# A ring of half pieces, a fifth pair by seven products, and results added to the residual by transfers, in one encoder layer

## The chip, the cores and the metric

The kernel runs on one core of a Trainium2 chip. Its engines work side by side, each through its own list of instructions in order: TensorE (PE, with PEld for its weight loads), VectorE (DVE), ScalarE (ACT), GpSimd (POOL) and SyncE (SP), which here only issues DMA transfers. The metric is the device time of one execution in microseconds (us), as a median of several runs. The profile is one execution, recorded instruction by instruction.

## The reference, cut to what matters

One encoder layer for 256 tokens of width 2048, float32 throughout:

```
h = rms_norm(x);  proj = h @ w_in                  # queries, keys, values, two gates
merged = sigmoid(ga) * (ya @ w_branch_a) + sigmoid(gb) * (yb @ w_branch_b)   # ya, yb: two attentions
x = x + merged @ w_out
hf = rms_norm(x);  g = dwconv3(hf @ w_ffn_gate)
x = x + (gelu(g) * (hf @ w_ffn_up)) @ w_ffn_down   # inner width 5632
x = x + sigmoid(rms_norm(x) @ w_ple_gate) * (p @ w_ple_proj)
out = rms_norm(x)
```

The change bears mostly on the product with `w_ffn_down`, 5632 rows by 2048 columns.

## The kernel before, in words

**Weights.** All weights are cut into blocks of 128x128, put on the host into the order in which they are used (`_stream`), and packed 16 to a *piece* of 1 MB; 263 pieces stream in on SP's queue (`load`, L198) into a ring of three buffers named `raw` (24 KB of each partition). `split_to` (L205) turns eight blocks at a time into two tensors for the matmuls: ACT rounds them to `whi` (L217), and DVE subtracts to get the remainder `wlo` (L218). Each has four buffers, and `split_to` runs three or four groups ahead of PE. A product is then three matmuls, high by high, high by low and low by high (L267 to L269, L311 to L313), which keeps float32's accuracy; the narrower products use two (L244, L245).

**Order.** The layer is a list of *jobs* (`_plan`): projections, attention, the `o` job in four quarters, then twice (for each half of the inner width) 22 gate and 22 up jobs and two *down* jobs `d0` or `d1`, one for each half of the 2048 columns; then four small `pp` jobs and four `pg` jobs. `at(...)` hangs small work (transposes, normalisation) on a step of a job, and `run_due` issues it there. A scheduler at compile time then fixes each engine's order from its own estimates, so that instructions of an engine can be moved against each other; `keep` holds an instruction in the order of the program.

**Down jobs.** A down job (`seven_product`, L288) takes its 22 rows of blocks in 11 pairs; a pair is one piece of weights, 2 rows by 8 columns of blocks, and two token halves. A normal pair takes eight block products of 512 columns, 24 matmuls. A *saved* pair takes seven, in the way of Strassen and Winograd, 21 matmuls. For it `combine` (L222) makes four differences of weight blocks on DVE (L229, L233, L234; the tile `spare`), so that such a pair has 28 blocks to split instead of 16, in four groups; and `add_up` makes four sums of activations (tiles `a32`, `s32`, then `shl`) after the eighth up job, for all four pairs in one go. `ORDER` puts four saved pairs (0 to 3) between seven normal ones: 4, 0, 5, 1, 6, 2, 7, 3, 8, 9, 10. When the last saved pair is done, `spread_sums` (L721) takes four PSUM banks into the residual with one ACT copy and eight DVE additions (L728); at the job's end `joined` (L776) adds the other four banks to the residual, each by a DVE instruction, and in `d1` ACT squares each quarter (L781) for the next norm.

**After the down jobs.** `flip` transposes the residual on PE (L745) and scales it into two halves on ACT (L367) and DVE (L368). `pp` copies its results on ACT (L702). Before `pp` job 2 the last gain is loaded by ACT's queue (L876). `gate` (L787 to L792) closes each quarter; `finish` sums the squares (L798), scales the sum (L387), raises it to -0.5 on POOL (L389), multiplies and stores (L802 to L807).

Of the kernel before, what the change touches and what calls it, by code (L numbers as in the profile page):

```python
# [111 lines left out]
ORDER = [4, 0, 5, 1, 6, 2, 7, 3, 8, 9, 10]  # L112
SAVED = 4
# [8 lines left out]
def _stream():  # L122

    blocks = [(j[2], j[4] + k, j[3]) for k in range(KC) for j in _JOBS[:FIRST]]
    for _, _, name, n, k0, count in _JOBS[FIRST:]:
        if isinstance(n, tuple) and len(n) == 8:
            for m in ORDER:
                if m < SAVED:
                    _SEVEN.add(len(blocks))
                blocks += [(name, k0 + 2 * m + e, c) for e in range(2) for c in n]  # L130
# [11 lines left out]
def _splits():  # L142

    subs = [(int(a), n, None) for a, n in zip(np.cumsum([0, 1, 2, 4, 4]), (1, 2, 4, 4, 5))]
# [13 lines left out]
def _encoder(ctx: ExitStack, tc, xt, pt, cols, table, onehot, mask, ident_in, last_gain, wts, xrows, out):  # L158
# [36 lines left out]
    def load(r, a=0, b=PIECE):  # L195
        if a == 0:
            raws[r] = wpool.tile([P, PIECE, P], F32, name="raw", bufs=3)
        nc.sync.dma_start(raws[r][:, a:b, :], wts[r].rearrange("p (b n) -> p b n", n=P)[:, a:b, :])  # L198
        state["raw"] = r + 1

    def load_all(i):
        while state["raw"] < min(i, _NPIECES):
            load(state["raw"])

    def split_to(i):  # L205
        while state["sub"] < min(i, len(_SUBS)):
            s = state["sub"]
            a, n, part = _SUBS[s]
            r, o = divmod(a, PIECE)
            load_all(r + 3)  # L210
            src = raws[r][:, o:o + n, :]
            if part is not None:
                src = combine(src, part)
# [8 lines left out]
    def combine(b, part):  # L222

        if part == 0:
            state["turn"] = turn = 1 - state.get("turn", 1)
            state["t"] = held["spare"][:, turn * PIECE * P:(turn + 1) * PIECE * P].rearrange("p (b n) -> p b n", n=P)
            four = b.rearrange("p (q b) n -> p q (b n)", q=4)
            t13 = state["t"][:, :8, :].rearrange("p (q b) n -> p q (b n)", q=2)
            nc.vector.tensor_tensor(t13, four[:, 1::2], four[:, :2], op=ALU.subtract)  # L229
            return b[:, 8:, :]  # L230
        if part == 1:
            t1, t2, t4 = (state["t"][:, c:c + 4, :] for c in (0, 8, 12))
            nc.vector.tensor_tensor(t2, b[:, 12:, :], t1, op=ALU.subtract)  # L233
            nc.vector.tensor_tensor(t4, b[:, 8:12, :], t2, op=ALU.subtract)  # L234
            return state["t"][:, :8, :]
        return state["t"][:, 8:, :] if part == 2 else b[:, :4, :]
# [51 lines left out]
    def seven_product(i, still, sums, tags, done):  # L288
# [14 lines left out]
        for m in ORDER:  # L303
            for name in ("p2", "p3", "p4") + (("p1", "p5", "p6", "p7") if m < SAVED else ("p2", "p3", "p4", "c22", "c22")):
# [14 lines left out]
        for m in ORDER:  # L319
            b = state["at"]  # L320
            s, _ = _SUB_OF[b]
            if m < SAVED:
# [7 lines left out]
            for e, steps in enumerate(each):  # L330
                if m >= SAVED or e % 2 == 0:
# [8 lines left out]
            if m == SAVED - 1:  # L340
# [96 lines left out]
    hba = big.tile([P, QH, AW], F32, name="hba", tag="b0", bufs=1)  # L437
    hbb = big.tile([P, BH, BW], F32, name="hbb", tag="b1", bufs=1)
# [4 lines left out]
    order = [(0, 1), (0, 0, 1), (0, 1, 3), (0, 3, 7), (1, 2), (0, 7, 11), (0, 11, PIECE), (2, 3)]  # L443
# [57 lines left out]
    def bias(h0, n):  # L501

        if h0 < QH:
            dst, lines = hba[:, h0:h0 + n, :], [[1, P]]
# [25 lines left out]
    def scores(heads, y):  # L530
# [17 lines left out]
        a, step = (hba[:, h, :], P) if n == 1 else (hbb[:, h - QH, :], 1)  # L548
# [75 lines left out]
    def after(job, i, acc, u=None):  # L624
# [66 lines left out]
        elif kind == "u":  # L691
# [3 lines left out]
            v = held["a32"][:, f, :] if f < 2 * SAVED else u  # L695
            nc.vector.tensor_tensor(v, u, held.pop(("gelu", n)), op=ALU.mult)
            halves(held["act"][:, f, :], v)
            if f == 2 * SAVED - 1:
                add_up()
# [4 lines left out]
    def add_up():  # L704

        a = held["a32"].rearrange("p (m e) (t n) -> p m e t n", e=2, t=2)
        a11, a12, a21, a22 = a[:, :, 0, 0], a[:, :, 1, 0], a[:, :, 0, 1], a[:, :, 1, 1]
        s = held["s32"]
# [4 lines left out]
        hi, lo = held["shl"][:, 0], held["shl"][:, 1]  # L713
        for c in (slice(0, 2), slice(2, 4)):
            nc.scalar.activation(hi[:, c], s[:, c], AF.Copy)
            nc.vector.tensor_tensor(lo[:, c], s[:, c], hi[:, c].bitcast(F32), op=ALU.subtract)
# [4 lines left out]
    def spread_sums(n, bank):  # L721

        q = [[res[:, t, (2 * n + c) * W4:(2 * n + c + 1) * W4] for c in range(2)] for t in range(2)]
        u = held["ff"].tile([P, W4], F32, name="sq4")
        v = held["ff"].tile([P, W4], F32, name="gate", bufs=2)

        def add(dst, a, b):
            nc.vector.tensor_tensor(dst, a, b, op=ALU.add)  # L728

        nc.scalar.activation(u, bank["p1"], AF.Copy)  # L730
        add(q[0][0], u, q[0][0])
        add(u, bank["p6"], u)
        add(v, bank["p7"], u)
        add(u, bank["p5"], u)
        add(q[1][0], v, q[1][0])
        add(v, bank["p5"], v)
        add(q[0][1], u, q[0][1])
        add(q[1][1], v, q[1][1])
# [22 lines left out]
    def merge(n, e, m):  # L761
# [6 lines left out]
        hi, lo = (held["merged"][k // SUB][:, k % SUB:k % SUB + 2, c:c + T] for c in (0, T))  # L768
# [3 lines left out]
    def joined(n, t, acc, scale, parts):  # L772
# [6 lines left out]
        if parts is not None:  # L779
# [204 lines left out]
```

## Time and profile before

| | us |
|---|---|
| median of 3 runs (lowest to highest) | 1480.47 (1480.2 to 1480.53) |
| the profiled execution | 1477.88 |
| its span, from the first to the last instruction | 1476.1 |
| PE busy in it | 1462.2 |
| DVE, ACT, POOL busy | 1065.5, 760.5, 3.7 |
| down jobs of the first half, first to last matmul's start | 888.99 to 1004.46 |
| down jobs of the second half | 1249.22 to 1365.34 |

The profile names an engine, the line of the kernel, and output and inputs by tile. The granted TensorE clock is 0.997 of full speed. In the rows of the timeline the first number is the start in us from the span's start, the second the duration; the bracket at the end gives idle time of that engine just before and what ended it. A busy time of PE counts modelled ends, since matmuls overlap; the distance between the starts of two matmuls is their pace.

### The profile page before, as it was taken

What the parts mean: (1) busy time and instruction counts of PE and PEld (TensorE: products, weight loads), DVE (VectorE), ACT (ScalarE), POOL (GpSimd) and SP (SyncE); (2) the same over time, 40 slices, a digit from 0 to 9 for tenths busy, and PEclk for the clock granted to TensorE, in tenths of its full rate; (3) what the DMA queues carried; (4) which work ended last, traced back from release to release, by engine and by line L of the source; (5) the groups of instructions that cost most, each with busy time, mean ns of one, the idle gap of its engine ahead of it and who ended that gap; (6) DMA issues with size and microseconds to landing.
All of it is one profiled execution on the core that took longest, in us unless ns stands there. A gap on an engine that the chain in (4) does not pass through costs nothing. (4 is left out here: it accounts for less than half of the span.)

```text
span 1476.1 us, 19530 instructions
## 1 busy us (share of the span) xinstructions
PE 1462.2 (99%) x7570; PEld 1248.4 (85%) x7570; DVE 1065.5 (72%) x1530; ACT 760.5 (52%) x1072; POOL 3.7 (0%) x9
## 2 busy tenths in 40 slices
PE   9999999999999999999999999999999999999997
PEld 8888888888888888888888888888888888888886
DVE  7686664664554555568898888887889888898565
ACT  7465444444444444555555555554555555655643
POOL 0000000000000000000000000000000000000000
PEclk9999999999999999999999999999999999999998
DMA  9644444445555554545455454555455454555552
GB/s 321 245 156 171 169 171 171 171 177 194 204 197 192 202 207 180 198 171 197 178 196 196 180 196 171 205 223 192 183 196 189 184 198 172 201 200 216 211 188 97
DMA packets 46375, 282.88 MB, mean 192 GB/s; under 512 B 5124, under 2 KB 9988, under 8 KB 14028
## 3 DMA queue, kind: packets, MB, share of 16 engines
q1 hardware_dynamic: 44268, 277.31, 50.8%
q10 hardware_dynamic: 2016, 4.33, 1.1%
q8 instruction: 59, 0.97, 0.2%
q14 instruction: 32, 0.26, 0.0%
HBM read 279.49 MB, written 2.14 MB: 191 GB/s over the span
## 5 line engine op out<-in xcount | busy, mean ns | idle before, releaser
L218 DVE TENSOR_TENSOR wlo<-raw,whi 128x1024 fp32r<-128x1024 f32 (+2 forms) x519 | 622.1, 1201 | 355.6 <-ACT whi L217 352.4
L217 ACT ACTIVATE whi<-raw 128x1024 fp32r<-128x1024 f32 (+2 forms) x519 | 541.1, 1043 | 605.5 <-PE acc L269 224.9
L244 PE MATMUL acc<-mov,whi 128*128 128x512 f32 x1840 | 641.9, 393 | 0.3 <-DVE mov L368 0.3
L245 PE MATMUL acc<-mov,wlo 128*128 128x256 f32 x1840 | 512.8, 279 | 0.0
L244 PEld LDWEIGHTS acc<-mov,whi 128*128 128x128 f32 x1840 | 344.7, 187 | 77.6 <-DVE mov L368 0.6
L245 PEld LDWEIGHTS acc<-mov,wlo 128*128 128x128 f32 x1840 | 346.7, 188 | 0.4
L268 PE MATMUL acc<-wlo,mov 128*128 128x512 f32 (+1 forms) x512 | 196.5, 384 | 0.5 <-DVE wlo L218 0.5
L267 PE MATMUL acc<-whi,mov 128*128 128x512 f32 (+1 forms) x512 | 196.8, 385 | 0.0
L269 PE MATMUL acc<-whi,mov 128*128 128x512 f32 (+1 forms) x512 | 196.4, 384 | 0.0
L267 PEld LDWEIGHTS acc<-whi,mov 128*128 128x128 f32 x512 | 96.7, 189 | 19.3 <-DVE wlo L218 0.8
L268 PEld LDWEIGHTS acc<-wlo,mov 128*128 128x128 f32 x512 | 96.7, 189 | 19.0 <-DVE wlo L218 0.9
L269 PEld LDWEIGHTS acc<-whi,mov 128*128 128x128 f32 x512 | 96.7, 189 | 18.8
L312 PE MATMUL acc<-wlo,act 128*128 128x512 f32 x272 | 106.3, 391 | 0.8 <-DVE wlo L218 0.8
L311 PE MATMUL acc<-whi,act 128*128 128x512 f32 x272 | 106.1, 390 | 0.0
L313 PE MATMUL acc<-whi,act 128*128 128x512 f32 x272 | 105.9, 389 | 0.0
L312 PEld LDWEIGHTS acc<-wlo,act 128*128 128x128 f32 x272 | 51.1, 188 | 12.0 <-DVE wlo L218 1.7
L311 PEld LDWEIGHTS acc<-whi,act 128*128 128x128 f32 x272 | 51.1, 188 | 10.7
L313 PEld LDWEIGHTS acc<-whi,act 128*128 128x128 f32 x272 | 51.1, 188 | 10.5
L267 PE MATMUL acc<-whi,merged 128*128 128x512 f32 x128 | 50.6, 396 | 0.0
L269 PE MATMUL acc<-whi,merged 128*128 128x512 f32 x128 | 49.9, 390 | 0.0
L268 PE MATMUL acc<-wlo,merged 128*128 128x512 f32 x128 | 49.8, 389 | 0.0
L217 ACT ACTIVATE whi<-spare 128x1024 fp32r<-128x1024 f32 x32 | 33.7, 1054 | 27.0 <-PE acc L313 26.2
(177 smaller groups left out, 1373.0 us busy)
## 6 DMA issues: line engine op xcount, KB each, us to landing
raw<-in_wts SPq DMA_DIRECT2D x251, 1024.0 KB, 4.8
raw<-in_wts SPq DMA_DIRECT2D x12, 512.0 KB, 7.4
x<-in_xrows ACTq DMA_DIRECT2D x8, 256.0 KB, 5.3
x<-in_xt SPq DMA_DIRECT2D x13, 128.0 KB, 6.6
hbb<-hold SPq DMA_DIRECT2D x3, 514.0 KB, 6.3
hba<-hold SPq DMA_DIRECT2D x2, 768.0 KB, 7.1
end<-in_last_gain ACTq DMA_DIRECT2D x1, 1024.0 KB, 4.8
out<-x ACTq DMA_DIRECT2D x2, 384.0 KB
```

What stands on the lines that cost most here:

```text
L217: nc.scalar.activation(hi, src, AF.Copy)
L218: nc.vector.tensor_tensor(lo, src, hi.bitcast(F32), op=ALU.subtract)
L244: nc.tensor.matmul(acc, hi[:, o, :], m, start=first, stop=False, skip_group_check=True)
L245: nc.tensor.matmul(acc[:, T:], lo[:, o, :], m[:, :T], start=False, stop=last, skip_group_check=True)
L267: nc.tensor.matmul(acc, xh, hi, start=(k == 0), stop=False)
L268: nc.tensor.matmul(acc, xh, lo, start=False, stop=False)
L269: nc.tensor.matmul(acc, xl, hi, start=False, stop=(k == n - 1))
L311: nc.tensor.matmul(acc, xh, hi, start=(e == 1), stop=False)
L312: nc.tensor.matmul(acc, xh, lo, start=False, stop=False)
L313: nc.tensor.matmul(acc, xl, hi, start=False, stop=(e == uses[name]))
```

## The change

It has these parts:

1. **The ring.** `raw` becomes six buffers of half a piece (8 blocks, 512 KB). Every piece is loaded by two transfers, and a buffer is free when its own eight blocks are split. `split_to` asks for half pieces five ahead of the one that it splits, six in the later groups of a saved pair. In a saved pair the second row's blocks now come first in the stream, so that the first half piece (`b2`) is one whole group; `combine` makes all four differences at the first group, from both halves, as four DVE instructions of 512 columns. Its target `spare` becomes two tiles of one piece each. The first piece is split as 1, 2, 5, 4, 4 blocks instead of 1, 2, 4, 4, 5.
2. **A fifth saved pair** in both `d0` jobs and in the first `d1` job, in the order 5, 0, 6, 1, 7, 2, 8, 3, 4, 9, 10. The second `d1` job keeps four. `add_up` now runs pair by pair, on tiles of the new ring `row` (seven buffers of 128x512).
3. **Results by transfers.** `spread_sums` copies one bank on ACT, adds three others on DVE with four instructions, and gives its four results to `to_residual`: a DMA issued by POOL that adds a 128x512 tile to the residual in SBUF. In the three jobs with five saved pairs the four results at the job's end go the same way, after a copy by ACT. In the last job two of the first four results and all of the last four are still added by DVE. The squares of the first `d1` job move to step 10 of the second, and all squares are kept in program order on ACT.
4. **Room.** The bias tables and the tile `merged` are cut differently between two buffers (`b0` smaller, `b1` larger).
5. **Small work.** Transposes of `merge` and `flip` that came at two steps come at one (steps 3, or 17 and 19; after the last down job, step 0 of the second `pp` job and step 1 of the third). The last gain is multiplied by the root of 2048 on DVE before `pp` job 3; the sum of three quarters' squares is made early (`so_far`), and `finish` adds the fourth's with one instruction in place of the sum and the scaling.

The diff, cut to its core:

```diff
+SAVED = 5
+SPLIT = 4
+ROWS = 7
+def _pairs(kind, c):
+    if kind == "d1" and c == 1:
+        return [4, 0, 5, 1, 6, 2, 7, 3, 8, 9, 10], 4
+    return [5, 0, 6, 1, 7, 2, 8, 3, 4, 9, 10], 5
...
     def load(r, a=0, b=PIECE):
-        if a == 0:
-            raws[r] = wpool.tile([P, PIECE, P], F32, name="raw", bufs=3)
-        nc.sync.dma_start(raws[r][:, a:b, :], wts[r].rearrange("p (b n) -> p b n", n=P)[:, a:b, :])
-        state["raw"] = r + 1
+        src = wts[r].rearrange("p (b n) -> p b n", n=P)
+        for h in range(a // SUB, -(-b // SUB)):
+            c, d = max(a - h * SUB, 0), min(b - h * SUB, SUB)
+            if c == 0:
+                raws[2 * r + h] = wpool.tile([P, SUB, P], F32, name="raw", bufs=6)
+            nc.sync.dma_start(raws[2 * r + h][:, c:d, :], src[:, h * SUB + c:h * SUB + d, :])
+            state["raw"] = 2 * r + h + 1
...
-            load_all(r + 3)
+            load_all(h + 6 + bool(part))
...
-    def combine(b, part):
+    def combine(b2, b1, part):
         if part == 0:
+            t = state["t"] = held["spare"][turn]
+            (b21, b22), (b11, b12) = [[b[:, :4, :], b[:, 4:, :]] for b in (b2, b1)]
+            t1, t3, t2, t4 = (t[:, c:c + 4, :] for c in range(0, PIECE, 4))
+            for dst, p, q in ((t1, b12, b11), (t3, b22, b12), (t2, b22, t1), (t4, b21, t2)):
+                nc.vector.tensor_tensor(dst, p, q, op=ALU.subtract)
+        return (b2, state["t"][:, :8, :], state["t"][:, 8:, :], b1[:, :4, :])[part]
...
+    def to_residual(n, t, c, a):
+        keep(nc.gpsimd.dma_start(quarter(n, t, c), a, accum_op=ALU.add))
+    def spread_sums(n, bank, end):
+        u = row()
         nc.scalar.activation(u, bank["p1"], AF.Copy)
+        to_residual(n, 0, 0, u)
+        last = u
+        for name in ("p6", "p7"):
+            v = row()
+            nc.vector.tensor_tensor(v, bank[name], last, op=ALU.add)
+            last, u = v, last
+        u, v = u, last
+        to_residual(n, 1, 0, v)
+        w = row()
+        nc.vector.tensor_tensor(u, bank["p5"], u, op=ALU.add)
+        nc.vector.tensor_tensor(w, bank["p5"], v, op=ALU.add)
+        for t, a in enumerate((u, w)):
+            if end:
+                q = quarter(n, t, 1)
+                nc.vector.tensor_tensor(q, q, a, op=ALU.add)
+            else:
+                to_residual(n, t, 1, a)
...
-                joined(2 * n + c, t, acc[name], 1.0, held["ss2"] if kind == "d1" else None)
+                if kind == "d1" and n:
+                    joined(2 * n + c, t, acc[name], 1.0, held["ss2"])
+                else:
+                    a = row()
+                    nc.scalar.activation(a, acc[name], AF.Copy)
+                    to_residual(n, t, c, a)
+                    if kind == "d1":
+                        at((i + 1, 10), squares_of, c, t, held["ss2"])
```

More of the change, by code (lines that the diff above doesn't have):

```diff
@@ L718, in summed, with row @@
     def summed(m, e):
         return [held["shl"][:, c, e, m, :] for c in range(2)]
[L721 to L738, printed above, removed]
+    def row():
+        return held["ff"].tile([P, W4], F32, name="row", bufs=ROWS)
```

143 lines of the change are left out of this document (75 added, 68 removed).

## The prediction

> **What bounds the kernel now.** I read the page first, then the stretches of the down jobs, then the single waits. The page's first part:
>
> ```profile
> span 1476.1 us, 19530 instructions
> ...
> PE 1462.2 (99%) x7570; PEld 1248.4 (85%) x7570; DVE 1065.5 (72%) x1530; ACT 760.5 (52%) x1072; POOL 3.7 (0%) x9
> ```
>
> PE is the bound, but its busy time is modelled, so the pace is read from the starts. Inside a down job (a quarter of L311 to L313):
>
> ```profile
> 913.74 0.39 PE L312 MATMUL acc<-wlo,act 128*128 128x512 f32 x1
> ...
> 919.63 0.39 PE L311 MATMUL acc<-whi,act 128*128 128x512 f32 x1
> 920.45 0.50 PE L312 MATMUL acc<-wlo,act 128*128 128x512 f32 x1 [0.43 <-DVE wlo L218]
> 920.79 0.39 PE L313 MATMUL acc<-whi,act 128*128 128x512 f32 x1
> ```
>
> From 913.74 to 919.63 lie 26 steps: 0.2265 us a matmul of 512 columns, whatever its row says of its own length. The next two steps are 0.82 and 0.34: 0.71 lost to a wait for DVE. So time goes only in two ways: fewer matmuls, or fewer waits of PE. The waits list names the large waits in the down jobs and what is behind them:
>
> ```profile
> DVE spare L229 <- DMA raw<-in_wts: 3.9, 5, 1.4
> ...
> PEld acc L312 <- DVE wlo L218: 1.7, 2, 0.9
> ```
>
> There are two such stops of PE. What led to the first stands in DVE's timeline:
>
> ```profile
> 904.62 1.23 DVE L229 TENSOR_TENSOR spare<-raw 128x1024 f32<-128x1024 f32 x1
> 905.76 0.69 DVE L218 TENSOR_TENSOR wlo<-raw,whi 128x512 fp32r<-128x512 f32 x1
> 906.36 0.69 DVE L233 TENSOR_TENSOR spare<-raw,spare 128x512 f32<-128x512 f32 x1
> 907.08 0.69 DVE L234 TENSOR_TENSOR spare<-raw,spare 128x512 f32<-128x512 f32 x1
> 907.69 3.58 DVE L218 TENSOR_TENSOR wlo<-raw,whi 128x1024 fp32r<-128x1024 f32 x3
> 911.19 1.22 DVE L218 TENSOR_TENSOR wlo<-spare,whi 128x1024 fp32r<-128x1024 f32 x1
> 913.44 1.23 DVE L218 TENSOR_TENSOR wlo<-spare,whi 128x1024 fp32r<-128x1024 f32 x1 [1.03 <-ACT whi L217]
> 916.10 1.23 DVE L229 TENSOR_TENSOR spare<-raw 128x1024 f32<-128x1024 f32 x1 [1.44 <-DMA raw<-in_wts]
> ```
>
> DVE was free at 914.66, but the piece of the next saved pair had not landed until 916.10; everything behind it on DVE moved back, and PE stood at 920.45. The piece takes the buffer of the normal pair, whose two remainders are the first two of the three at 907.69. Overlapped, a 1024-wide DVE step costs 1.14 us (904.62 to 905.76), a 512-wide one 0.60, so that buffer was free at 907.69 + 2 x 1.14 = 909.97. The landing row of line 198 in this stage fits:
>
> ```profile
> DMA to landing us min/median/max: 4.7/4.8/6.1
> ```
>
> 909.97 + 6.1 is 916.1. A last large stop stands where the gate job starts:
>
> ```profile
> 1378.67 1.08 ACT L702 ACTIVATE end<-acc 128x512 f32<-128x512 f32 x2
> 1379.62 1.07 ACT L217 ACTIVATE whi<-raw 128x1024 fp32r<-128x1024 f32 x1
> ...
> 1380.72 1.23 DVE L218 TENSOR_TENSOR wlo<-raw,whi 128x1024 fp32r<-128x1024 f32 x1 [1.44 <-ACT whi L217]
> ```
>
> ```profile
> 1381.10 0.39 PE L267 MATMUL acc<-whi,mov 128*128 128x512 f32 x1
> 1382.00 0.50 PE L268 MATMUL acc<-wlo,mov 128*128 128x512 f32 x1 [0.52 <-DVE wlo L218]
> 1382.34 0.40 PE L269 MATMUL acc<-whi,mov 128*128 128x512 f32 x1
> ```
>
> Steps of 0.90 and 0.34 there: 0.79 lost, because ACT's rounding of those weights stood behind two copies of line 702.
>
> **Fewer matmuls.** A normal pair takes 8 x 3 = 24 matmuls, a saved one 7 x 3 = 21. Counts over the two jobs of the first half:
>
> ```profile
> L312 PE MATMUL acc<-wlo,act 128*128 128x512 f32 x136 | 53.2, 391 | 0.8 <-DVE wlo L218 0.8
> ...
> L312 PE MATMUL acc<-wlo,shl 128*128 128x512 f32 x32 | 12.4, 389 | 0.0
> ```
>
> 168 here, as many on L311 and L313: 504, or 4 x 21 + 7 x 24 = 252 a job. With five saved pairs it is 249. Three jobs: nine matmuls, 9 x 0.2265 = **2.04 us**, certain if PE stays fed.
>
> **Does DVE keep up?** Busy time of the two jobs, and of a stretch of the gate and up jobs (after the window: its length, PE, PEld, DVE, ACT, POOL, clock, DMA share, GB/s):
>
> ```profile
> 889.00:946.00 57.00, 56.57 (x251) 46.48 (x250) 49.63 (x57) 30.87 (x33) 0.00 (x0) 1.00 0.55 202
> 946.00:1004.00 58.00, 57.62 (x254) 47.39 (x253) 48.50 (x53) 30.19 (x31) 0.00 (x0) 1.00 0.54 203
> ```
>
> ```profile
> 660.00:880.00 220.00, 220.00 (x1272) 193.97 (x1271) 184.57 (x325) 115.36 (x182) 0.00 (x0) 1.00 0.52 191
> ```
>
> A new saved pair costs DVE four 512-wide steps, two of them dependent (0.72 as 906.36 to 907.08), so 2.6; then three remainders of 1.14 and one of 0.60: 6.6 in all, against 2.3 for the normal pair it replaces: +4.3. The sums after the last saved pair fall from nine to four (-3.0), and four additions into the residual leave DVE (-2.4). Sum -1.1: about 48.5 of 56.3 us. On ACT, 1.5 more roundings (1.6 us) and four copies that replace DVE's additions:
>
> ```profile
> L776 DVE TENSOR_TENSOR x<-acc,x 128x512 f32<-128x512 f32 x6 | 3.9, 684 | 1.1 <-PE acc L313 1.1
> ...
> L730 ACT ACTIVATE sq<-acc 128x512 f32<-128x512 f32 x2 | 1.2, 582 | 0.0
> ```
>
> 4 x 0.58 makes 34.8 of 56.3 for ACT. Both keep cover. In the gate and up jobs the sums of a pair come one pair at a time. Each of four 128x128 additions lies between 0.16 (the 128x1 rows of the tail below) and 0.68 (the 512-wide row); I take 0.25, which with a 512-wide remainder is 1.7 us a pair, 8.5 for five; the block it replaces was 4 x 0.68 + 2 x 1.2 = 5.1. DVE is idle for 35 of 220 us there, so I count nothing; at 0.68 it would be 17 in 250, still covered.
>
> **The ring.** The second half piece of a saved pair now waits only for its own 512 KB. Rows:
>
> ```profile
> raw<-in_wts SPq DMA_DIRECT2D x251, 1024.0 KB, 4.8
> raw<-in_wts SPq DMA_DIRECT2D x12, 512.0 KB, 7.4
> x<-in_xrows ACTq DMA_DIRECT2D x8, 256.0 KB, 5.3
> ...
> out<-gate SPq DMA_DIRECT2D x2, 256.0 KB, 2.5
> ```
>
> Between 2.5 for 256 KB and 4.8 for 1 MB, 512 KB is some 3.3 us, an estimate (7.4 was at the start, with many queued). The first half's buffer is free at 908.83, the second's at 909.97: landed by 913.3 (914.8 at 4.8). DVE reaches the combination at 914.66, so neither makes it wait. Both stops then go: 0.71 and, for the second, which has the same cause by the waits list, about 0.65: **-1.35**. What is late next is PE's own pace. SP issues twice as many transfers, 44 in 116 us at about 0.35 each: hidden.
>
> The Trainium skill ("DMA: Bandwidth & Descriptors", section "Rules for kernel authors") asks for 1 MiB or more in one DMA, which speaks against half pieces. Its fit, 2.0 us plus bytes at 436 GB/s, gives 3.2 for 512 KB, and the 4.8 row for 1 MB lies near its 4.4; by the rule alone the sum would be that of rival 4.
>
> **Two saved pairs in a row.** Pairs 3 and 4 are adjacent: DVE needs 6.6 us for pair 4 while PE spends 21 x 0.2265 = 4.76 on pair 3. That is 1.85 short, and DVE's lead covers it if the combination is issued early, as L229 is (ahead of the previous pair's last remainder at 905.76). Bounds 0 and 3 x 1.85 = 5.5; nearest to the timeline is little, **+0.3**.
>
> **Results by transfer.** 26 transfers of 256 KB, issued by POOL, which is otherwise idle; eight in each of three jobs, two in the last. Issue and landing aren't in this trace; by the 256 KB rows one takes 2.5 to 5.3 us. They add 2.1 MB to some 11.5 MB a job, a DMA share of 0.55 to perhaps 0.7. First to wait are ACT's four squares at step 10 of the last job: from the last saved pair until then PE has two normal pairs (10.9), then three normal and two saved ones (25.8): 36.7 us for eight transfers, 4.6 each if one after another. At 3.3 they are done: **0**. The ring of seven rows is reused a job later, and is covered likewise.
>
> **Start of the gate job.** Flips one and three move forward by up to one small job, so their transposes and ACT copies no longer stand before the rounding; against it DVE gains the multiplication of the last gain. 2048 wide, by
>
> ```profile
> L806 DVE TENSOR_SCALAR x<-x,rr 128x768 f32<-128x768 f32 x2 | 1.2, 612 | 0.0
> ...
> L802 DVE TENSOR_SCALAR gate<-gate,rr 128x512 f32<-128x512 f32 x2 | 1.0, 487 | 1.5 <-POOL rr L389 1.5
> ```
>
> 0.125 more for 256 columns gives 1.2 us (0.6 to 2.4). It also waits for its 1 MB transfer, and may hold up remainders behind it. Bounds -0.79 and +2; I take half the stop, **-0.40**. Elsewhere flips and merges are regrouped, with as many transposes: nothing.
>
> **Tail.**
>
> ```profile
> 1469.41 0.16 DVE L798 TENSOR_REDUCE sum<-marks 128x1 f32<-128x4 f32 x1
> 1469.60 0.16 DVE L387 TENSOR_SCALAR rv<-sum 128x1 f32<-128x1 f32 x1
> ```
>
> One small addition in place of both: **-0.19**, on the path. More queues to close at the end: 0 to 0.5, I take **+0.1**. Chunks at the start are cut otherwise, with the same bytes ahead of the same blocks: nothing.
>
> **Sum.** -2.04 - 1.35 + 0.30 - 0.40 - 0.19 + 0.10 = -3.58. The profiled execution took 1477.88, span 1476.06; it becomes 1474.3. The runs' median is 2.59 above the profiled time; keeping that, 1480.47 - 3.6 = **1476.9 us**.
>
> **Rivals.**
> 1. *The matmuls go, the waits stay* (half pieces land no earlier, or an equal stop comes elsewhere). For it: DVE is 86% busy in these jobs. Against: the 1.4 us between 914.66 and 916.10. -2.04 - 0.19 = 1478.2.
> 2. *Adjacent saved pairs starve PE*, up to +5.5: 1477 to 1482.4, most likely 1479.5. For it: 6.6 against 4.76. Against: the order seen at 904.62.
> 3. *Slow transfers make it slower.* Place: ACT's squares in the last job, behind which weight roundings queue; PE lives on four buffers of 6 to 12 matmuls, some 6 us. From about 5.3 us a transfer, one after another, this decides (8 x 5.3 = 42.4 against 36.7 + 6); at 7 us PE stands 13 us: 1490. For it: no row of such a transfer exists, and 5.3 is a measured row for this size. Against: that row's eight loads ran beside weights, and transfers to different quarters need not go one after another. The Trainium skill ("SBUF — State Buffer", "Who interferes with whom") says that descriptors for DMAs issued from GpSimd are held up while VectorE runs in a two-port mode, but not by tensor_tensor; by that rule the down jobs, whose DVE rows are all TENSOR_TENSOR, would escape, and no run here shows it yet.
> 4. *Half pieces move one after another*: 2 x 3.3 a piece against 5.2 us of matmuls, 1.4 late on each of 263 pieces: about 1840. Against it is a stretch near the start, in which the twelve transfers of 512 KB were the largest:
>
> ```profile
> 10.00:20.00 10.00, 9.18 (x52) 7.78 (x53) 8.00 (x12) 8.72 (x13) 0.00 (x0) 1.00 1.02 391
> ```
>
> 391 GB/s, more than twice what 512 KB in 3.3 us give (159): they run side by side.
>
> **How the numbers follow.** This kernel's measurement can tell about 0.2% from no change: below 1477.51 is faster, above 1483.43 slower. Forecast 0.53: with every gain and no loss the sum is -2.04 - 1.35 - 0.79 - 0.19 = -4.4, 1476.1, and 0.6 below that stands for terms taken as nothing: 1475.5; above, 1478.0 (mostly below the bound), rival 1 0.18, rival 2 0.14, rival 3 0.13, rival 4 0.02. Faster: 0.42 of the forecast, 0.03 of rivals 1 and 2: 0.45. Same: 0.11 + 0.16 + 0.13 = 0.40. Slower: 0.15. The range from 1475.5 to 1482.4 holds all but rivals 3 and 4.
>
> **What would show it.** 249 matmuls in three jobs; no wait of DVE for raw in them, and no PE step over 0.4 us; DVE about 48 us a job; the transfers' landing below 4.6 us; step sizes around the first remainder of pair 4; the start of the gate job. It is wrong if PE's waits grow past 2 us anywhere, most of all behind ACT's squares.

## The result and the profile after

| | us |
|---|---|
| before, median of 6 runs beside it (lowest to highest) | 1480.22 (1477.75 to 1480.53) |
| after, median of 6 runs (lowest to highest) | 1488.14 (1485.87 to 1490.53) |
| ratio after to before, 95% interval | 1.0058 [1.0045, 1.0071] |
| the profiled execution after, its span | 1489.59, 1487.7 |
| down jobs of the first half, before and after | 115.5 and 118.6 |
| down jobs of the second half, before and after | 116.1 and 125.0 |

The change makes the kernel slower by 0.58%, 8.6 us by the ratio. The forecast was 1476.9, the range ended at 1482.4. The profiled executions lie further apart (11.7 us) than the medians, since that of before was near its quickest run and that of after above its median; in what follows stops are counted in the profiled executions and sizes are taken from the ratios.

The page of after, its totals, queues and transfers:

```profile
span 1487.7 us, 20288 instructions
...
PE 1463.7 (98%) x7561; PEld 1246.8 (84%) x7561; DVE 1071.0 (72%) x1577; ACT 771.7 (52%) x1096; POOL 26.7 (2%) x35
...
q1 hardware_dynamic: 80412, 277.33, 56.9%
q0 software_dynamic: 3744, 6.82, 2.5%
...
raw<-in_wts SPq DMA_DIRECT2D x514, 512.0 KB, 4.7
x<-row POOLq DMA_DIRECT2D x26, 256.0 KB, 7.5
```

PE has 7561 matmuls where it had 7570: nine fewer, as intended, at the same pace of 0.227 us. DVE's total is 1071.0 after 1065.5. So no engine has much more to do, and the time is in waits. After's list of waits (engine and line, what it waited for, us in total, times, longest):

```profile
DVE ta L247 <- DMA raw<-in_wts: 19.8, 10, 5.5
PEld acc L324 <- DVE wlo L235: 17.7, 16, 2.3
...
PE acc L324 <- DVE wlo L235: 11.4, 13, 1.8
DVE tb L247 <- DMA raw<-in_wts: 11.2, 9, 2.6
```

L247 makes the four differences of a saved pair, in tile `ta` or `tb` in turn; L235 is the remainder (L218 before). Before had 3.9 us of the first kind in 5 waits and 1.7 of the second in 2. Now DVE stands still 31.0 us for half pieces, and PE for DVE. From the starts of the matmuls there are 13 stops of PE of over 0.25 us in the down jobs, 13.5 us in all, and none of that size from there to the end of the kernel. Each is followed by a step 0.11 longer, so 15.0 us. With nine matmuls fewer (2.0) and the two stops of before gone (1.4), that is +11.6 of the 12.0 us by which the four jobs grew in the profiled executions.

The first half's two jobs (after the window: its length, PE, PEld, DVE, ACT, POOL, clock, DMA share, GB/s):

```profile
889.00:946.00 57.00, 56.34 (x248) 45.95 (x247) 49.98 (x61) 32.95 (x37) 2.79 (x3) 1.00 0.61 196
946.00:1007.00 61.00, 57.60 (x250) 46.40 (x250) 48.58 (x55) 33.76 (x38) 7.02 (x8) 1.00 0.76 222
```

DVE works 98.6 us in the first two jobs, 98.1 before: it isn't overloaded. What moved is the order of its work and the time at which its data come. DVE's timeline of after, between two saved pairs:

```profile
903.27 1.23 DVE L235 TENSOR_TENSOR wlo<-tb,whi 128x1024 fp32r<-128x1024 f32 x1 [0.66 <-ACT whi L234]
905.86 1.29 DVE L247 TENSOR_TENSOR ta<-raw 128x512 f32<-128x512 f32 x2 [1.36 <-DMA raw<-in_wts]
907.07 0.69 DVE L235 TENSOR_TENSOR wlo<-raw,whi 128x512 fp32r<-128x512 f32 x1
907.67 1.41 DVE L247 TENSOR_TENSOR ta<-raw,ta 128x512 f32<-128x512 f32 x2
909.00 3.49 DVE L235 TENSOR_TENSOR wlo<-raw,whi 128x1024 fp32r<-128x1024 f32 x3
```

and on to the next one, with SP's issue between them:

```profile
911.27 1.22 DVE L235 TENSOR_TENSOR wlo<-raw,whi 128x1024 fp32r<-128x1024 f32 x1
...
911.38 0.33 SPq L213 DMA_DIRECT2D raw<-in_wts  x1
...
916.58 1.29 DVE L247 TENSOR_TENSOR tb<-raw 128x512 f32<-128x512 f32 x2 [1.16 <-DMA raw<-in_wts]
```

This is a **closed loop**, and it can be read off row by row. The differences wait for the later half of their pair (905.86). Behind them on DVE stand the remainders of the normal pair (the first two of the three merged at 909.00: 909.00 and 910.13), though PE needs those first. The second of these ends at 911.27 and frees a buffer; SP issues the later half of the *next* saved pair into it at 911.38; it lands 5.2 us on, and the next differences start at 916.58. The DVE part is 3.14 + 2.27, the issue 0.11, the landing 5.2: 10.72 us a turn. In one turn PE does a normal and a saved pair, 45 x 0.2265 = 10.19. So it falls behind by half a microsecond, and PE stops:

```profile
909.46 0.39 PE L323 MATMUL acc<-whi,act 128*128 128x512 f32 x1
910.27 0.50 PE L324 MATMUL acc<-wlo,act 128*128 128x512 f32 x1 [0.43 <-DVE wlo L235]
```

A landing of 4.7 us (10.19 less 5.52) is the limit. The half pieces' landing between 896 and 936 us lies across it:

```profile
DMA to landing us min/median/max: 3.7/4.8/5.6
```

Four half pieces are asked for within 3.4 us (898.09, 899.23, 900.36, 901.50) and land after 3.8, 5.2, 5.5 and 5.6 us: only the first is alone. The worst stops come while transfers run. DVE's timeline in the last down job:

```profile
1312.51 0.69 DVE L247 TENSOR_TENSOR tb<-raw,tb 128x512 f32<-128x512 f32 x1
1318.70 1.29 DVE L247 TENSOR_TENSOR ta<-raw 128x512 f32<-128x512 f32 x2 [5.50 <-DMA raw<-in_wts]
1319.91 1.22 DVE L235 TENSOR_TENSOR wlo<-tb,whi 128x1024 fp32r<-128x1024 f32 x1
```

DVE stands for 5.50 us at a difference whose half piece took 8.4 us (issued at 1310.29). The remainder of `tb` behind it was ready: ACT had rounded those weights at 1313.9. PE waited for just that remainder:

```profile
1318.96 0.39 PE L323 MATMUL acc<-whi,shl 128*128 128x512 f32 x1
1321.18 0.50 PE L324 MATMUL acc<-wlo,shl 128*128 128x512 f32 x1 [1.83 <-DVE wlo L235]
```

The DMA engines in that stretch, 1300 to 1320 us (tenths of their time in 40 slices, then the queues, the median landing):

```profile
DMA  4988899344776688999999999999999999999999
...
q1 hardware_dynamic: 1144, 4.18, 59.3%
q0 software_dynamic: 685, 1.26, 34.2%
...
raw<-in_wts SPq DMA_DIRECT2D x7, 512.0 KB, 8.0
x<-row POOLq DMA_DIRECT2D x7, 256.0 KB, 7.5
```

They are full. The Trainium skill ("DMA: Bandwidth & Descriptors", section "Rules for kernel authors") says that spreading DMAs over SP, ACT and GpSimd brings no bandwidth, because all run on the same 16 engines and interleave. The trace agrees: half pieces land in 8.0 us here and in 4.7 over the whole kernel.

### The profile page after: what moved, and what is told of

Its sections match the earlier page's. It is cut to its first block, busy times and chain, and to the rows that moved or that the text cites. A ratio compares the mean times of both kernels' runs of the same rounds, so it can differ in the third digit from the quotient of the medians.

```text
span 1487.7 us, 20288 instructions
## 1 busy us (share of the span) xinstructions
PE 1463.7 (98%) x7561; PEld 1246.8 (84%) x7561; DVE 1071.0 (72%) x1577; ACT 771.7 (52%) x1096; POOL 26.7 (2%) x35
## 3 DMA queue, kind: packets, MB, share of 16 engines
q1 hardware_dynamic: 80412, 277.33, 56.9%
q0 software_dynamic: 3744, 6.82, 2.5%
## 4 chain that ended last, share of the span: by engine, by line
PE 46%; issue 40%; DMA 7%; DVE 6%; ACT 1%; SPq 0%; POOL 0%; DVEq 0%; POOLq 0%; ACTq 0%
PE acc L256 20%; PE acc L257 10%; DMA raw<-in_wts 6%; DVE wlo L235 4%; PE acc L279 2%; PE acc L280 2%; PE acc L281 2%; PE acc L324 2%; PE acc L325 2%; PE acc L323 2%; PE first L256 1%; DVE ta L247 1%; DVE tb L247 1%; PE first L257 1%; DMA x<-in_xt 0%
## 5 line engine op out<-in xcount | busy, mean ns | idle before, releaser
L235 DVE TENSOR_TENSOR wlo<-raw,whi 128x1024 fp32r<-128x1024 f32 (+2 forms) x519 | 619.0, 1197 | 343.1 <-ACT whi L234 341.6
L234 ACT ACTIVATE whi<-raw 128x1024 fp32r<-128x1024 f32 (+2 forms) x519 | 539.2, 1040 | 603.2 <-PE acc L281 231.9
L324 PE MATMUL acc<-wlo,act 128*128 128x512 f32 x257 | 101.4, 394 | 7.0 <-DVE wlo L235 7.0
L323 PE MATMUL acc<-whi,act 128*128 128x512 f32 x257 | 100.3, 390 | 0.0
L325 PE MATMUL acc<-whi,act 128*128 128x512 f32 x257 | 100.3, 390 | 0.0
L324 PEld LDWEIGHTS acc<-wlo,act 128*128 128x128 f32 x257 | 48.2, 188 | 21.3 <-DVE wlo L235 11.6
L323 PEld LDWEIGHTS acc<-whi,act 128*128 128x128 f32 x257 | 48.3, 188 | 10.1
L325 PEld LDWEIGHTS acc<-whi,act 128*128 128x128 f32 x257 | 48.3, 188 | 9.6
L363 ACT ACTIVATE t<-acc 128x256 f32<-128x256 f32 x115 | 41.9, 364 | 0.0
```

Of the source, the lines that this page charges most:

```text
L234: nc.scalar.activation(hi, src, AF.Copy)
L235: nc.vector.tensor_tensor(lo, src, hi.bitcast(F32), op=ALU.subtract)
L323: nc.tensor.matmul(acc, xh, hi, start=(e == 1), stop=False)
L324: nc.tensor.matmul(acc, xh, lo, start=False, stop=False)
L325: nc.tensor.matmul(acc, xl, hi, start=False, stop=(e == uses[name]))
L363: keep(nc.scalar.activation(t, acc[:, T:], AF.Copy, scale=scale))
```

## The experiments

The theory: the loop above. Its parts are an order of DVE in which differences stand ahead of remainders that are ready, and a landing that is longer than the loop allows. Rivals: the half pieces are slow by themselves; the transfers' load is what costs; DVE or ACT has too much work. "Before" is run beside each group: 1479.78 (e1 to e4), 1479.68 (e5 to e8), 1478.79 (e9 to e12); compare by ratio.

| | what | median us | ratio, 95% |
|---|---|---|---|
| after | halves, transfers, order moved | 1488.14 | 1.0058 [1.0045, 1.0071] |
| e1 | after, three whole pieces | 1487.67 | 1.0051 [1.0034, 1.0068] |
| e2 | after, no transfers | 1485.53 | 1.0041 [1.0026, 1.0056] |
| e8 | after, whole pieces, no transfers | 1476.47 | 0.9978 [0.9969, 0.9988] |
| e3 | before with the six halves | 1483.51 | 1.0033 [1.0021, 1.0045] |
| e9 | e2 with eight halves | 1479.26 | 0.9999 [0.999, 1.0008] |
| e4 | after, differences in program order | 1474.09 | 0.9965 [0.9952, 0.9978] |
| e6 | e4, no transfers | 1475.33 | 0.9971 [0.9959, 0.9983] |
| e7 | e4, three whole pieces | 1474.14 | 0.9961 [0.9948, 0.9973] |
| e12 | e4 with four saved pairs everywhere | 1475.52 | 0.9977 [0.9968, 0.9986] |
| e10 | e4 with five saved pairs everywhere | 1475.93 | 0.9979 [0.997, 0.9988] |
| e11 | e10, three whole pieces | 1475.55 | 0.9977 [0.9968, 0.9987] |
| e5 | before, differences in program order | 1476.65 | 0.998 [0.9971, 0.9989] |

**e1, the ring undone.** Three whole pieces again; the pairs, differences and transfers of after stay.

```diff
-            if c == 0:
-                raws[2 * r + h] = wpool.tile([P, SUB, P], F32, name="raw", bufs=6)
-            nc.sync.dma_start(raws[2 * r + h][:, c:d, :], src[:, h * SUB + c:h * SUB + d, :])
+        if a == 0:
+            raws[r] = wpool.tile([P, PIECE, P], F32, name="raw", bufs=3)
+        nc.sync.dma_start(raws[r][:, a:b, :], wts[r].rearrange("p (b n) -> p b n", n=P)[:, a:b, :])
...
-            load_all(h + 6 + bool(part))
+            load_all(r + 3)
```

> The changed kernel with the ring of three whole pieces put back; five saved pairs and the transfers stay. Three theories. Ring: half pieces are issued four in a burst, land 5.2 to 5.6 us after their issue instead of the 3.3 that I took, and the four differences wait for the second half on VectorE, in front of work that is ready; those stops of TensorE in the alternating part of the four down jobs (some 9 us of the profiled execution) fall back to the 1 to 2 of before: 1481 to 1483. Transfers: the stops at the start of a job that follows eight transfers (5 us, 954 to 957 and 1321 to 1324) stay, with DVE's single waits of over 4 us there. Load of VectorE (rival): the fifth pair with four differences in a block is too much, and waits for DMA only mark it: 1487 to 1489, no change.

Measured: 1.0051, within the interval of after. The waits of e1:

```profile
PEld acc L319 <- DVE wlo L230: 14.9, 16, 1.9
DVE ta L242 <- DMA raw<-in_wts: 11.9, 5, 3.5
DVE tb L242 <- DMA raw<-in_wts: 9.3, 5, 2.7
```

The same kind of wait, 10 instead of 19 but longer on average; the first stop of PE comes at 955.55, after the first transfers, none before. So small pieces alone are not the cause.

**e2, the transfers undone.** Every result is added to the residual by DVE again.

```diff
-        to_residual(n, 0, 0, u)
+        add(q[0][0], u, q[0][0])
...
-                if kind == "d1" and n:
-                    joined(2 * n + c, t, acc[name], 1.0, held["ss2"])
-                else:
-                    a = row()
-                    nc.scalar.activation(a, acc[name], AF.Copy)
-                    to_residual(n, t, c, a)
+                joined(2 * n + c, t, acc[name], 1.0, held["ss2"] if kind == "d1" else None)
```

> The changed kernel with the results added by VectorE again (nine instructions after the last saved pair, four at the job's end), ring of half pieces and five saved pairs as changed. Transfers theory: the stops at the start of the second job of each half go, about -5 us: 1482 to 1484; half pieces there land within 5.6 us instead of 7 to 8.7. Ring theory: the stops in the alternating part stay. Load theory: VectorE gets 5.4 us more in each of three jobs, so the time is 1489 or more.

Measured: 1.0041. Removing the transfers alone brings back less than a third (0.17%, inside the intervals). The largest waits of e2 (another of 10.9 us, of `ta`, stands between these):

```profile
PEld acc L324 <- DVE wlo L235: 12.0, 14, 1.9
...
DVE tb L247 <- DMA raw<-in_wts: 8.3, 9, 1.9
```

The four stops that after has at the start of a second down job (954.86, 957.32, 1321.18 and 1323.65, 5.0 us in all) are gone, as the theory of load has it. But ten stops of PE over 0.25 us remain while saved and normal pairs alternate (and one at the end of the second job). Three of them (900.73, 911.87, 922.72) lie earlier than the first transfer of after, at 937.3. So the transfers' load alone is not the cause either.

**e3, the ring alone.** Before with six halves and the new `combine`, no fifth pair, no transfers.

```diff
-            raws[r] = wpool.tile([P, PIECE, P], F32, name="raw", bufs=3)
+                raws[2 * r + h] = wpool.tile([P, SUB, P], F32, name="raw", bufs=6)
...
+            for dst, p, q in ((t1, b12, b11), (t3, b22, b12), (t2, b22, t1), (t4, b21, t2)):
+                nc.vector.tensor_tensor(dst, p, q, op=ALU.subtract)
```

> The kernel before with the ring of six half pieces alone (second row's blocks first, all four differences at the first group); four saved pairs, no transfers. Ring theory: more and longer stops for landed halves, 2 to 6 us slower than before: 1482.5 to 1486. Load and transfers theories: as before, 1479.5 to 1481. What I forecast on record, that the ring takes the two stops away, would give 1479.

Measured: 1.0033, slower than before. DVE waits 17.2 us for halves (3.9 before), PE stops eight times in the down jobs, and a stop of 0.68 at the gate job's start stays. The part from which the prediction took 1.35 us costs 4.9.

**e4, the order.** After, with the four differences held in the order of the program: one word.

```diff
-                nc.vector.tensor_tensor(dst, p, q, op=ALU.subtract)
+                keep(nc.vector.tensor_tensor(dst, p, q, op=ALU.subtract))
```

> The changed kernel with one difference: the four differences of a saved pair are kept in the order of the program on VectorE, behind the remainders that come before them, instead of being moved ahead of them at compile time. If the stops come from VectorE waiting for a half piece in front of work that is ready, they nearly go in the alternating part (-7 or more): 1478 to 1481, and those at the start of a job shrink. If the halves are simply too late for the matmuls, or VectorE has too much to do, no change: 1487 to 1489.

Measured: 0.9965. With all of its parts, the change is 0.35% faster than before once DVE's order is kept, and 0.93% faster than as made. DVE's timeline of e4, at the place shown of after:

```profile
905.94 0.69 DVE L235 TENSOR_TENSOR wlo<-raw,whi 128x512 fp32r<-128x512 f32 x1
907.65 2.54 DVE L235 TENSOR_TENSOR wlo<-raw,whi 128x1024 fp32r<-128x1024 f32 x2 [1.03 <-ACT whi L234]
910.11 1.28 DVE L247 TENSOR_TENSOR ta<-raw 128x512 f32<-128x512 f32 x2
```

Now the last remainder of the old pair and the two of the normal pair come first. The buffer is free before the differences start, and its half piece is needed a whole turn later: a landing may take about 10 us, and in the full stretch some come near that. The DMA engines of e4 from 1290 to 1314 us:

```profile
DMA  9632598779997889999999999999999999999999
...
raw<-in_wts SPq DMA_DIRECT2D x10, 512.0 KB, 7.4
x<-row POOLq DMA_DIRECT2D x8, 256.0 KB, 8.0
```

and the waits of e4:

```profile
DVE ta L247 <- DMA raw<-in_wts: 1.4, 1, 1.4
...
PEld acc L324 <- DVE wlo L235: 1.1, 4, 0.3
```

As full, half pieces as late (7.4 in the median, one of 9.97), and yet one wait of DVE and no stop of PE over 0.25 us in the down jobs. That ends the theory that the load costs by itself. The same section of the Trainium skill advises to issue a DMA early and wait for it late; the order in after waits for it early, and in program order 31.0 us of DVE's waits become 1.4.

**e5, the order in the kernel before.** The same word on L229, L233 and L234.

```diff
-            nc.vector.tensor_tensor(t13, four[:, 1::2], four[:, :2], op=ALU.subtract)
+            keep(nc.vector.tensor_tensor(t13, four[:, 1::2], four[:, :2], op=ALU.subtract))
```

> The kernel before, with the three instructions that make the differences of weights kept in the order of the program on VectorE; nothing else changed. Loop theory: the differences of pair C wait for a piece that goes into the buffer of the normal pair n, whose second remainder stands on VectorE behind the differences of the pair before; from the start of one group of differences to the next this loop takes the landing plus 5.4 us of VectorE, against 10.2 us of matmuls. At 4.75 us of landing it is level, at 6.1 it stops TensorE. In order, the remainders come first, the loop is cut, and the two stops of before (1.35 us) go: 1478.0 to 1479.3 against about 1480. Rival, that the order matters only beside half pieces and transfers: no change, 1479.6 to 1480.3.

Measured: 0.998, 3.0 us, more than the two stops of the profiled execution (1.4). Before sits at the edge of the same loop: 904.62 to 909.97 on DVE is 5.35, and with the median landing of a whole piece, 4.8, a turn takes 10.15 against 10.19. Landings at 6.0 and 6.1 (pieces issued at 910.07 and 967.79) push it over, once for each of its two stops. That other executions of before have more such stops than the profiled one fits its medians, but no trace shows it. e4 is a further 0.15% below e5, about the worth of the nine matmuls, though the two intervals overlap: most of what e4 gains on before is the order.

**e6, e7, e8: the parts, in order and not.** e6 is e4 with e2's edit, e7 is e4 with e1's edit, e8 is after with both edits but DVE's order as it falls.

> The changed kernel with the differences in order, and the results added by VectorE instead of by transfers. Loop theory: with the loop cut, transfers neither cost nor give much; VectorE gets 5.4 us more in each of three jobs (54 of 56 us busy), so small stops may come back: 1474 to 1476.5. If the transfers are what still costs in the run with the differences in order (landings of 8 us), 1472 to 1473.5.

> The changed kernel with the differences in order and three whole pieces as ring; five pairs and transfers stay. Loop theory: 1473.8 to 1475.5, the ring's cut is worth little either way once the loop is cut. Rival, that the half pieces are what lets the data be there in time: the first saved pair after eight transfers stops TensorE again, 1477 or more.

> The changed kernel without the ring of half pieces and without transfers: of the three large parts the fifth saved pair alone is left, with its four differences as a block at the first group, moved ahead by the scheduler as in the changed kernel. Loop theory: whole pieces land as before, so the stops stay near before's (1 to 4 us in all) and nine matmuls go: 1478 to 1481. Load theory (the fifth pair is too much for VectorE): 1484 or more.

Measured: 0.9971, 0.9961 and 0.9978. In order, halves against whole pieces makes no difference (e4 and e7), and the transfers bring some 0.06%, 0.9 us, inside the intervals; a stop of 1.29 us in e6 at the end of the second down job, which e4 hasn't, is of that size. e6 also tests the rival of too much work, since DVE has its additions back. Its first two down jobs (columns as above):

```profile
888.00:945.00 57.00, 57.00 (x253) 46.94 (x252) 53.42 (x67) 32.62 (x35) 0.00 (x0) 1.00 0.61 198
945.00:1002.00 57.00, 56.63 (x250) 46.37 (x248) 54.24 (x65) 32.32 (x34) 0.00 (x0) 1.00 0.63 204
```

DVE works 107.7 of 114 us, 9 more than in the slower kernel after, and PE has no stop over 0.25 us inside the jobs: DVE's load is not the cause.

Out of order the parts don't add up: on e8 the halves cost 0.63% (e2), the transfers 0.73% (e1), both together 0.80%. Each by itself goes with landings over the limit, but not for one reason. In e2's down jobs DVE waits over 1 us for eight half pieces; they landed after 4.6 to 6.8 us, six of them after 5.3 or more. In e1's it waits so for seven whole pieces, which took 6.5 to 8.5 us; packets of the transfers were moving beside four of them and none beside the other three (issued at 969.80, 1272.46 and 1335.18). So e1's 0.73% is not all due to pieces that transfers held up. e8 stays near the limit, with whole pieces at 4.8 us in the median, and has two stops in the alternating part, 1.18 and 0.76, and one of 1.18 at the end of the second down job, which e2, e6 and e9, the other kernels without transfers, have as well. DVE waits 6.3 us for raw in it, in 6 waits.

**e9, a deeper ring without the order.** e2 with two more half buffers from the gate jobs on; the ring `row`, which no transfer uses here, shrinks from seven buffers to three. The scheduler also spreads the later differences singly between the remainders; the first still stand ahead.

```diff
+                more = held.get("ff") and (2 * r + h) % 4 == 3
+                raws[2 * r + h] = (held["ff"].tile([P, SUB, P], F32, name="raw2", bufs=2) if more else
+                                   wpool.tile([P, SUB, P], F32, name="raw", bufs=6))
...
-            load_all(h + 6 + bool(part))
+            load_all(h + (8 if held.get("ff") else 6) + bool(part))
```

> The changed kernel with its results added by DVE (e2), and two more buffers for half pieces in the FFN stage alone: eight halves instead of six, each half asked for two releases earlier. The order is not written out; DVE's stream comes out with the differences still ahead of ready remainders (the first ones of each saved pair ahead of the remainder s3, the others singly between the remainders), so an early difference still stands before work that could run. Everything is computed. Theory (a closed loop: the landing of a half plus DVE's work behind it sets the pace, because the buffer is freed by a remainder that stands behind the waiting difference): with two halves more in hand the landing no longer lies in the loop, so the stops of TensorE in the alternating part go, all 11 of e2 to at most two: 1485.5 less 8 to 10 = 1475.5 to 1477.5 us, and DVE's waits for raw fall from 19 us to under 5. Rival (the wait for the landing itself is what costs, wherever the difference stands ahead of ready work, and the ring's depth decides nothing): 1484 to 1486 us, DVE's waits for raw still above 15 us.

Measured: 0.9999, against 1.0041 for e2: 6.2 of the 8 to 10 us foreseen, and in the alternating part three stops over 0.25 us instead of ten, two of 1.53 and one of 0.28. With the first differences still ahead, a deeper ring takes most of the stops away, which speaks for the loop from its other side. It is no clean test: the order of the later differences changed too, the time lies between what the loop (1475.5 to 1477.5) and its rival (1484 to 1486) foresaw, and DVE's waits fell to 13.6 us, not under 5. What is left is partly order without any landing; DVE's timeline of e9 at one of the two larger stops:

```profile
919.23 0.68 DVE L249 TENSOR_TENSOR ta<-raw 128x512 f32<-128x512 f32 x1
919.83 0.68 DVE L249 TENSOR_TENSOR ta<-raw,ta 128x512 f32<-128x512 f32 x1
920.44 3.48 DVE L237 TENSOR_TENSOR wlo<-raw,whi 128x1024 fp32r<-128x1024 f32 x3
```

Three differences of the next saved pair, 0.6 us each (the first at 918.02), stand before a remainder whose weights ACT had rounded at 917.68, and PE stands until 921.71. Eight buffers beside the transfers, which take seven buffers of `row`, weren't tried.

**e10, e11, e12: how many pairs.** e4 with the fifth pair in the last job too; the same with whole pieces; e4 with four everywhere.

```diff
-    if kind == "d1" and c == 1:
-        return [4, 0, 5, 1, 6, 2, 7, 3, 8, 9, 10], 4
     return [5, 0, 6, 1, 7, 2, 8, 3, 4, 9, 10], 5
...
-                                  [(i + 1, k) for k in (17, 17, 19, 19)]):
+                                  [(i + 1, k) for k in (19, 19, 21, 21)]):
```

> The kernel of e4 (changed kernel, differences in program order) with the fifth saved pair in the fourth down job too, and the sign changes of the saved rows two steps later in that job. Everything is computed. Three matmuls fewer at 0.2265 us. Theory (in order, nothing else binds): 0.68 us below e4, 1474.1 to 1473.4 us, no step of TensorE in the down jobs more than 0.25 us over its pace. Rival (this job is the one whose combination has the least cover, so a stop comes with it): 1474.1 to 1476 us, with a stop of TensorE in that job.

> The same with three whole pieces in the ring in place of six halves. Everything is computed. Theory (in order the ring is worth nothing, as e4 and e7 have it): equal to the six halves within 0.2%, 1473.4 us. Rival (six halves hide more of the landing in the job with the new pair): 0.7 to 1.4 us above the six halves.

> The kernel of e4 with four saved pairs in all four down jobs, so without the fifth; ring of six halves and transfers stay. Everything is computed. Nine matmuls more at 0.2265 us. Theory (in order, the fifth pair brings its matmuls and no wait): 1474.1 + 2.04 = 1476.1 us. Rival (adjacent saved pairs cost a wait that e4 hides in its total): less than 1 us above e4, 1474 to 1475 us.

Measured: 0.9979, 0.9977 and 0.9977. e12 is 0.12% or 1.8 us above e4. The two intervals overlap, but the profiled executions agree: the four down jobs take 230.1 us in e12 and 228.5 in e4, with no stop over 0.25 us in either. So the nine matmuls are worth 1.6 to 1.8 of the 2.04 us that they were priced at. The fifth pair in the last job was expected to bring 0.68 and costs about 2 (0.14%, where the intervals overlap too); beside e12, from the same group, e10 is no faster though it has twelve matmuls fewer. The two down jobs of the second half take 115.5 us, as in e4, with three matmuls fewer and a stop of 0.30 in them, and another of 1.10 comes later, at 1376.87. DVE's timeline of e10 there:

```profile
1373.32 0.87 DVE L378 SCALAR_TENSOR_TENSOR mov<-pt,cl,mov 128x256 fp32r<-128x256 f32 x2
1375.10 1.23 DVE L912 TENSOR_SCALAR end<-end 128x2048 f32<-128x2048 f32 x1 [0.91 <-DMA end<-in_last_gain]
1376.24 0.87 DVE L378 SCALAR_TENSOR_TENSOR mov<-pt,cl,mov 128x256 fp32r<-128x256 f32 x2
```

and PE's:

```profile
1375.54 0.39 PE L279 MATMUL acc<-whi,pw 128*128 128x512 f32 x1
1376.87 0.47 PE L277 MATMUL acc<-whi,mov 128*128 128x512 f32 x1 [0.94 <-DVE mov L378]
```

It is the pattern of the loop in small: the last gain's multiplication waits for its load, and the scaled residual that PE wants stands behind it. In e4 that load is issued 0.9 us earlier and all four `mov` steps come ahead of the multiplication. e11 has the same stop with whole pieces. The two stops less the three matmuls make some 0.8 of the 2 us; the rest was not traced.

## Why the prediction was wrong, point by point

- **Fewer matmuls** (2.04): right, 7561 in the trace, and 1.6 to 1.8 us by e12.
- **Does DVE keep up** (about 48.5 us a job): right in its size, 49.3 us a job in the first two. ACT was put at 34.8 and has 33.4. The rebuilt sums left the gate and up jobs without a stop.
- **The ring** (-1.35): this is the step that failed. It set "landed by 913.3 (914.8 at 4.8)" against a DVE that is at the combination at 914.66, with 3.3 us for 512 KB by interpolation; even its own 914.8 is later than 914.66, so "neither makes it wait" didn't follow, and the quoted row of 512 KB with many queued, 7.4, was set aside. The halves that matter take 5.2 to 5.5 in the first job; the first half and the next normal pair's are asked for just before and after, and only the first of the four, at 3.8, comes near 3.3. The fit that the prediction quotes from the Trainium skill ("DMA: Bandwidth & Descriptors", section "Anatomy of one DMA — SWDGE (gpsimd) path") is given there for transfers that GpSimd issues, and SP issues these. The second half's buffer is free no sooner than a whole piece's was, and differences need both halves, so the halves gained nothing. And the comparison was made once, with DVE's times held fixed, though the times it used (904.62, 909.97, 916.10) were one turn of a loop: in a loop the excess over 10.19 us comes back with every saved pair. Instead of -1.35 it is +4.9 on before (e3). With the order kept and the loop cut (e4), the change is at 0.9965 of before, a little below the forecast's 0.9976.
- **Results by transfer, 0**: failed with it. Each 256 KB lands in 7.5 us, not 3.3, and what is late is not ACT's squares but the weights. Load that costs nothing in order (e4) costs 0.17% here (after against e2, inside the intervals) and 0.73% between e8 and e1, where three of the seven late pieces had no transfer beside them.
- **Two saved pairs in a row** (+0.3): didn't come; by the count of matmuls these pairs stand at 926 to 936, 987 to 997 and 1292 to 1301 us, and none of the 13 stops lies there. The combination stands early enough, as the prediction said.
- **Start of the gate job** (-0.40): better than forecast; the stop of 0.79 is gone in after and e4, and stays in e3 and e5, which lack this part.
- **Tail** (-0.19 and +0.10): the last sum's step is right, from its start to that of the last multiplication of a quarter 0.90 us instead of 1.08. From there to the end of the span it is 6.41 us in after and 5.57 before, so +0.84 and not +0.10. The profiled executions with transfers lie at 6.1 to 6.4 there and those without at 5.6 to 5.8, but e6, without, at 6.3; the cause stays open.
- **Rivals**: rival 1's condition (half pieces land no earlier) is what happened, but it was priced as a stop that stays, not one that is repeated. Rival 3 had the right sign and the wrong place: ACT waited 0.4 us for the transfers. Rivals 2 and 4 did not come.

What the prediction could have seen: in the quoted rows of before, L229 at 904.62 already stood ahead of the three remainders at 907.69. It was taken as help for rival 2, an early combination, and it was the loop.

## What to carry to other kernels

When an engine works in order, look at what stands behind an instruction that waits for a load: if it is the work that frees the ring's buffer for the next load, landing and work add up to a loop, and its length against the consumer's pace per turn decides, not any engine's share. Price a load by its landing among its neighbours, not alone, and ask what longer landing the order can bear (here 4.7 us in one order and about 10 in the other). A part that is worth nothing or harmful in a kernel near such a limit says little of its worth: fix the order first, then measure the parts.

## What the runs showed of the hardware that was not expected

The transfers that add to the residual, in the rows of after for line 745 (duration of one issue in ns, least, median, most; then landing):

```profile
L745 POOL DMA_DIRECT2D x<-row x26: 869/872/1050, 937.3 to 1364.0; - x26
...
DMA to landing us min/median/max: 3.5/7.5/9.8
```

A transfer from SBUF to SBUF that adds takes POOL 0.87 us to issue, and in the full stretch from 1300 to 1320 us it used 34.2% of the engines' time for 1.26 MB where the weights used 59.3% for 4.18 MB: 27 against 14 per MB, 1.9 times the share for a byte (1.8 over the whole kernel, by 2.5% for 6.82 MB against 56.9% for 277.33). The weights in halves also cost the engines more: in a stretch of the gate and up jobs, where no transfer to the residual runs, after and then e8, with whole pieces:

```profile
660.00:880.00 220.00, 220.00 (x1271) 193.97 (x1271) 188.63 (x345) 115.86 (x185) 0.00 (x0) 1.00 0.60 190
```

```profile
660.00:880.00 220.00, 220.00 (x1271) 193.97 (x1270) 188.46 (x344) 115.63 (x184) 0.00 (x0) 1.00 0.54 191
```

A share of 0.60 against 0.54 for the same 190 GB/s. All runs with halves show 0.59 or 0.60 there, all with whole pieces 0.52 to 0.54.

Some pieces are late with no transfer beside them. The profile also has a DMA queue that it names instruction (q8), with 59 packets and 0.97 MB in the whole of before. In before's down jobs 30 weight pieces had no packet of it starting while they were under way, and landed after 4.65 to 4.96 us. Nine had one: six of these landed after 4.75 to 5.26, and three after 5.88, 6.01 and 6.08. The last two are the pieces behind the two stops of before, and the pieces behind e8's two stops in the alternating part (6.43 and 6.50) had one too, as had the three in e1. That such a packet delays a piece was not tested, and most that had one beside them were hardly late.
